# Two value blocks in one PSUM bank, and a norm's last square written to PSUM

## The chip, the cores and the metric

The kernel runs on one core of one Trainium2 chip. The metric is the device time of one execution in microseconds; lower is better. Several executions are timed and their median is given. Separately, one execution is taken with the hardware profiler, and the profile and the trace come from that one.

## The reference

Two layers of a bidirectional encoder over 512 tokens of width 1024, in float32. Each layer has three residual blocks, each behind an RMS norm:

```python
for l in range(DEPTH):
    x = x + hybrid_mixer(rms_norm(x, norm_mix[l]), w_in[l], ...)
    x = x + memory_cross_attention(rms_norm(x, norm_mem_q[l]), rms_norm(mem, norm_mem_kv[l]), ...)
    x = x + conv_ffn(rms_norm(x, norm_ffn[l]), w_up[l], conv_w[l], conv_b[l], w_down[l])
return rms_norm(x, norm_final)

def rms_norm(x, g):
    return x * lax.rsqrt(jnp.mean(x * x, axis=-1, keepdims=True) + EPS) * g
```

The mixer projects the normalised tokens once (`proj = h @ w_in`) into queries, keys and values. Eight heads of width 64 attend to a window of a 2-D grid of tokens (the neighbourhood heads), eight query heads on two key heads attend to all tokens (the grouped heads). One output product joins both. The memory block attends to 256 memory tokens with four heads, and the last block is a gated feed-forward layer with a convolution of width 3 over the positions.

## The kernel before

**Layout.** The tokens are kept transposed: `xT[c]` is a tile of 128 features by 512 tokens, and c runs over KC = 8 chunks. A product in float32 precision is made of three matmuls of a faster type: every operand is split into a hi part (a cast by ScalarE, ACT) and a lo part (the difference), and `mm3` adds hi x hi, hi x lo and lo x hi into one PSUM bank. So every weight that is loaded, and every result that is multiplied again, is split: ACT casts, and VectorE (DVE) or GpSimd (POOL) subtracts. Weights are split on line 742 (hi, ACT) and line 743 (lo, POOL, in a few cases DVE).

**PSUM.** There are eight banks of 128 x 512 values, given out in turn from three pools: four `mm` banks for products (`ps_mm`), two `sc` banks for scores (`ps_s`), two `tr` banks for transposes and small sums (`ps_t`). A tile of a pool takes the bank of the tile that came as many turns before, and has to wait until that one was used for the last time.

**A norm.** `Norm` does not wait for its statistic. Each closing product of the block before gives one chunk of the new x; `close` adds it into x (lines 978, 979), makes the split operands `xg` for the next product with the gain alone (lines 987, 989), and squares the chunk on ACT (line 995). POOL adds the squares up in SBUF, but the last chunk's (c = 7) is added by DVE (line 1006). `stat` then sums over the partitions with eight small matmuls (`tr<-ones,t`), and the rest of rsqrt follows on DVE (line 944) and POOL (line 946). `spread` brings rstd into a row form, and the results of the products are scaled with it when they are evicted (lines 1215, 1220 for q and k, lines 1037 and 1038 for the values). The very first norm, on the input, is built apart, with its squares added by DVE. The final norm has no gain column (`gcol is None`).

**The first products of a layer.** Their order is `NA_ORDER`: q and k of head pair 0, q and k of pair 1, then the value blocks of the first four heads (`project_v`), q and k of pairs 2 and 3, then one wide product for the other values and the keys of the grouped heads (`kv`), and one for their queries (`gq`). q and k of pair 0 use `sc` banks, all others `mm` banks. In layer 0 the three first products run interleaved while the input lands. `project_v` makes four blocks of 128 tokens by 256 columns; for each it takes one `mm` bank, of which it uses half, runs 24 matmuls and evicts the block with `split_v`. When all four are done, `straddle` copies halves of them by DMA into blocks that lie across the borders.

**The order of work.** The program is written as generators that a `Filler` interleaves, and PE's work is traced in that order. Then `Order` plans ACT, DVE, POOL and PE anew: it makes 30 rounds of a list schedule with estimated times, moves due times after each round by a seeded random draw, keeps the round that ended first, and pins the order of every engine to it. Transfers on SP's queue stay in the written order. In its estimates, DVE and POOL exclude each other where an operation "shares", and a DVE operation that reads a PSUM tile does not:

```python
if self.engine != "DVE" or what not in ("InstTensorTensor", "InstTensorScalarPtr") or self.banked(self.reads):
    return False
```

Two operations of different engines on one PSUM bank are kept one after the other, whichever columns they touch.

Of the kernel before, what the change touches and what calls it, by code (L numbers as in the profile page):

```python
# [19 lines left out]
P = 128  # L20
# [6 lines left out]
KC = D // P  # L27
# [628 lines left out]
def encoder_kernel(ctx: ExitStack, tc: tile.TileContext, t: dict, out: bass.AP):  # L656
# [17 lines left out]
    def nm(s):  # L674
        uid[0] += 1
        return f"{s}_{uid[0]}"
# [15 lines left out]
    def tmp(shape=(S,)):  # L692
        return tpool.tile([P, *shape], F32, tag="t", name=nm("t"))
# [4 lines left out]
    def ps(tag, bufs):  # L698
        return psum.tile([P, S], F32, tag=tag, name=nm(tag), bufs=bufs)

    ps_mm = lambda: ps("mm", 4)
    ps_s = lambda: ps("sc", 2)
    ps_t = lambda: ps("tr", 2)
# [91 lines left out]
    def get_w(key, ahead=AHEAD):  # L795
        n = done[0]
        assert plan[n][0] == key, (plan[n][0], key)
        prepare_w(1 + ahead)
        done[0] += 1
        w = ready[n]  # L800
        ready[n] = None
        return w
# [89 lines left out]
    def mm3(ps, ah, al, bh, bl, start, stop, **k):  # L892

        PE.matmul(ps, ah, bh, start=start, stop=False, **k)
        PE.matmul(ps, ah, bl, start=False, stop=False, **k)
        PE.matmul(ps, al, bh, start=False, stop=stop, **k)
# [66 lines left out]
    class Norm:  # L963
# [27 lines left out]

        def square(self, c, act=ACT, eng=None):

            sq = tmp((self.n,)) if self.gcol is not None or c == 0 or c >= KC - 2 else ps_s()[:, : self.n]
            e = act.activation(sq, xT[c][:, self.cols], AF.Square)
            eng = eng or (POOL if self.gcol is not None and c < KC - 1 else DVE)
            if self.acc is None:
                self.acc = sq
            elif c >= KC - 2 and self.gcol is None:
                self.last.append(sq)  # L1000
            elif c == 1:
                acc = tmp((self.n,))
                eng.tensor_add(acc, self.acc, sq)
                self.acc = acc
            else:
                eng.tensor_add(self.acc, self.acc, sq)  # L1006
            return e
# [24 lines left out]
    def split_psum(hi, lo, ps, scale=None):  # L1032
        if scale is None:
            ACT.copy(hi, ps)  # L1034
            DVE.tensor_sub(lo, ps, f(hi))  # L1035
        else:
            ACT.mul(hi, ps, scale)
            DVE.scalar_tensor_tensor(lo, ps, scale, f(hi), op0=ALU.mult, op1=ALU.subtract)
# [114 lines left out]
    for l in range(DEPTH):  # L1153
# [100 lines left out]
        vblk, straddled = [None, None], [False, False]  # L1254

        def v_blocks(g):
            vs = [rtile((2, 4, P)) for _ in range(4)]
            vblk[g] = {P * b: vs[b // 2][:, b % 2] for b in range(NB)}
            vblk[g].update({P * b + 64: vs[2 + b // 2][:, b % 2] for b in range(NB - 1)})
            return vs  # L1260
# [24 lines left out]
        def project_v(g):  # L1285

            w = [get_w(("v", g, kh)) for kh in range(2)]
            vs = v_blocks(g)
            for b in range(NB):
                pm = ps_mm()[:, :256]  # L1290
                bs = slice(b * P, b * P + P)
                for k in range(KC):
                    wh, wl = (v[:, k % 4, :] for v in w[k // 4])
                    mm3(pm, xg[k][0][:, bs], xg[k][1][:, bs], wh, wl, k == 0, k == KC - 1)
                    if k == 3:
                        yield
                split_v(vblk[g][P * b], pm, b)
                if b == NB - 1:
                    late(1, lambda: straddle(g, vs))
                yield  # L1300

        def split_v(v, pm, b):
            split_psum(v[:, :, 0:HD], v[:, :, HD:P], pm.rearrange("p (h d) -> p h d", d=HD), mix.rstd[:, b : b + 1])
# [17 lines left out]
        def straddle(g, vs):  # L1321
            straddled[g] = True
            for dst, src in (
                (vs[2][0:64, 0:2], vs[0][64:128, 0:2]),
                (vs[2][64:128, 0], vs[0][0:64, 1]),
                (vs[2][64:128, 1], vs[1][0:64, 0]),
                (vs[3][0:64, 0], vs[1][64:128, 0]),
                (vs[3][64:128, 0], vs[1][0:64, 1]),
            ):
                SP.dma_start(f(dst), f(src))  # L1330
# [311 lines left out]
        if l > 0:  # L1642
            load_bias(0)
        project = {"v": project_v, "kv": project_kv, "gq": lambda p: project_gq()}
        units = [project[n](p) if n in project else project_qk(n, p) for n, p in NA_ORDER]
        nns = []
# [444 lines left out]
```

## Time and profile before

| what | us |
|---|---|
| median of 3 runs | 1319.31 (1319.14 to 1320.14) |
| the profiled execution, its own time | 1318.48 |
| its span in the profile | 1316.7 |
| TensorE (PE) busy | 1303.8 |
| DVE busy | 1003.9 |
| ACT busy | 786.6 |
| POOL busy | 721.2 |

The granted TensorE clock is 0.999 of full speed. A row of the timeline has the start and the time in us, the engine, the line, the operation, the tiles (out<-in, without numbers), the shape and a count, and in brackets how long the engine was idle before it and what ended that. `tr<-ones,t` are the sums of a norm, `mm<-xg,hi` and `mm<-xg,lo` a projection, `mm<-hi,xg` and `mm<-lo,xg` a product in which the tokens are the stationary side, as in the value blocks. All matmuls stand under line 103, the helper that counts them.

### The profile page before, as it was taken

The page shows a single profiled execution, that of the slowest core. Times are in us where ns is not written, and L with a number is a line of the kernel's source. Part 1 is how long each engine was busy: PE and PEld are TensorE (multiplying, and loading weights), DVE is VectorE, ACT ScalarE, POOL GpSimd, SP SyncE. Part 2 cuts the span into 40 slices and gives each one's busy share as a digit, 9 for nine tenths or more (in the row PEclk, how much of TensorE's full clock was granted, in tenths as well). Part 3 has the DMA queues.
Part 4 walks back from the last instruction along what each step waited for, and adds up shares of the span by engine and source line. Part 5 has one row for each costly group of instructions (what it writes and reads, how often), then busy time and mean ns, then how long its engine had stood idle before and what let it go on. Part 6 is the DMA issues. An engine that isn't in the chain of part 4 may idle for free.

```text
span 1316.7 us, 21053 instructions
## 1 busy us (share of the span) xinstructions
PE 1303.8 (99%) x7632; PEld 1146.9 (87%) x7632; DVE 1003.9 (76%) x1858; ACT 786.6 (60%) x1458; POOL 721.2 (55%) x520
## 2 busy tenths in 40 slices
PE   9999999999999999999999999999999999999998
PEld 8888888888789999999888888888887999999987
DVE  6569877665999987788545688876759999877874
ACT  6768876555645555545536678765645555555544
POOL 3657966717464454445736569655454544444443
PEclk9999999999999999999999999999999999999999
DMA  7744322313223333333455523223222333333332
GB/s 239 199 118 134 97 80 65 96 48 112 75 70 105 109 108 101 97 95 102 138 147 166 146 78 100 62 78 95 64 84 85 88 90 105 105 98 90 110 104 76
DMA packets 205000, 136.98 MB, mean 104 GB/s; under 512 B 5600, under 2 KB 195040, under 8 KB 204896
## 3 DMA queue, kind: packets, MB, share of 16 engines
q1 hardware_dynamic: 204080, 134.98, 35.2%
q8 instruction: 60, 0.98, 0.3%
q10 hardware_dynamic: 816, 0.66, 0.2%
q14 instruction: 44, 0.36, 0.1%
HBM read 125.65 MB, written 2.10 MB: 97 GB/s over the span
## 4 chain that ended last, share of the span: by engine, by line
PE 89%; DVE 6%; ACT 2%; issue 1%; DMA 1%; POOL 0%; SPq 0%; POOLq 0%; DVEq 0%; ACTq 0%
PE mm L103 61%; PE sc L103 20%; PE tr L103 4%; PE tr L1537 2%; DVE t L1830 1%; DMA xT<-in_xT 1%; DVE t L1006 1%; PE tr L1382 1%; DVE r L1850 1%; PE tr L1724 1%; DVE r L1035 1%; DVE xg L1859 0%; DVE r L1252 0%; ACT t L1360 0%; ACT r L1034 0%
## 5 line engine op out<-in xcount | busy, mean ns | idle before, releaser
L743 POOL TENSOR_TENSOR lo<-raw,hi 128x512 fp32r<-128x512 f32 (+3 forms) x230 | 370.5, 1624 | 288.5 <-ACT hi L742 238.2
L103 PE MATMUL mm<-r,hi 128*128 128x512 f32 (+1 forms) x1392 | 396.5, 366 | 0.0
L103 PEld LDWEIGHTS mm<-r,hi 128*128 128x128 f32 x1392 | 245.3, 189 | 34.8
L103 PE MATMUL mm<-xg,hi 128*128 128x512 f32 (+1 forms) x960 | 267.3, 363 | 1.1 <-DVE xg L1859 0.3
L103 PE MATMUL mm<-r,lo 128*128 128x512 f32 (+1 forms) x728 | 257.5, 356 | 0.0
L742 ACT CAST hi<-raw 128x512 fp32r<-128x512 f32 (+3 forms) x234 | 167.8, 740 | 133.3 <-PE mm L103 45.3
L103 PEld LDWEIGHTS mm<-xg,hi 128*128 128x128 f32 x960 | 170.1, 189 | 30.2 <-DVE xg L1859 2.7
L103 PE MATMUL mm<-xg,lo 128*128 128x512 f32 (+1 forms) x480 | 173.5, 361 | 0.0
L103 PE MATMUL sc<-r,hi 128*128 128x256 f32 (+1 forms) x832 | 162.6, 291 | 0.0
L754 POOL TENSOR_TENSOR lo<-sf,hi 128x1024 fp32r<-128x1024 f32 x32 | 77.6, 2426 | 148.3 <-ACT hi L751 112.1
L103 PEld LDWEIGHTS mm<-r,lo 128*128 128x128 f32 x728 | 137.5, 189 | 19.8
L103 PEld LDWEIGHTS sc<-r,hi 128*128 128x128 f32 x832 | 133.8, 191 | 4.9
L103 PE MATMUL sc<-r,lo 128*128 128x256 f32 (+1 forms) x416 | 121.1, 291 | 0.0
L751 ACT CAST hi<-sf 128x1024 fp32r<-128x1024 f32 x64 | 67.2, 1049 | 86.7 <-DVE sf L766 47.2
L103 PE MATMUL mm<-hi,xg 128*128 128x512 f32 (+1 forms) x384 | 111.3, 360 | 1.3 <-DVE r L1252 1.3
L103 PEld LDWEIGHTS mm<-xg,lo 128*128 128x128 f32 x480 | 90.7, 189 | 13.8
L754 POOL TENSOR_TENSOR lo<-raw,hi 128x1024 fp32r<-128x1024 f32 x32 | 77.5, 2422 | 44.5 <-PE mm L103 25.0
L1041 POOL TENSOR_SCALAR t<-t,s 128x512 f32<-128x512 f32 (+1 forms) x112 | 66.5, 607 | 48.9 <-DVE s L1521 25.5
L103 PEld LDWEIGHTS sc<-r,lo 128*128 128x128 f32 x416 | 79.6, 191 | 1.2
L103 PEld LDWEIGHTS mm<-hi,xg 128*128 128x128 f32 x384 | 68.0, 190 | 10.5 <-DVE r L1252 1.5
L103 PE MATMUL sc<-r,r 128*128 128x256 f32 (+1 forms) x352 | 74.3, 330 | 0.0
L765 DVE TENSOR_TENSOR sf<-raw 128x512 f32<-128x512 f32 x32 | 62.7, 1960 | 8.2 <-DMA raw<-in_w_up 8.2
(200 smaller groups left out, 2629.6 us busy)
## 6 DMA issues: line engine op xcount, KB each, us to landing
raw<-in_w_up SPq DMA_DIRECT2D x88, 512.0 KB, 3.8
raw<-in_w_down SPq DMA_DIRECT2D x36, 384.0 KB, 3.5
raw<-in_w_in SPq DMA_DIRECT2D x25, 512.0 KB, 4.8
raw<-in_w_mem_kv SPq DMA_DIRECT2D x16, 512.0 KB, 4.3
raw<-in_w_down SPq DMA_DIRECT2D x24, 320.0 KB, 3.1
r<-in_bias SPq DMA_DIRECT2D x16, 384.0 KB, 5.3
r<-r SPq DMA_DIRECT2D x22, 256.0 KB, 3.4
raw<-in_w_in SPq DMA_DIRECT2D x18, 256.0 KB, 4.7
```

What stands on the lines that cost most here:

```text
L103: return self.engine.matmul(out, lhsT, rhs, **k)
L742: act.copy(hi[:, k], raw[:, k])
L743: (POOL if eng[0] == "P" else DVE).tensor_sub(lo[:, k], raw[:, k], f(hi)[:, k])
L751: act.copy(hi, src)
L754: eng.tensor_sub(lo[:, c], src[:, c], f(hi)[:, c])
L765: DVE.tensor_add(both[:, :4], raw[:, :4], raw[:, 4:])
L1006: eng.tensor_add(self.acc, self.acc, sq)
L1035: DVE.tensor_sub(lo, ps, f(hi))
L1041: eng.tensor_scalar(e, e, sums[:, col : col + 1], 1.0, op0=ALU.mult, op1=ALU.mult)
L1382: PE.transpose(tr[:, (2 * i + c) * P : (2 * i + c + 1) * P], es[j][:, i, c * P : (c + 1) * P], ident)
L1537: PE.transpose(tr[:, k * P : (k + 1) * P], es[j][:, k * P : (k + 1) * P], ident)
L1724: PE.transpose(tr[:, (2 * c + i) * P : (2 * c + i + 1) * P], e[:, i, c * P : (c + 1) * P], ident)
```

## The change

In `square`, the square of the last chunk is written to a `tr` bank in place of an SBUF tile, in every norm with a gain column but the very first. There are five of these: the memory norm and the feed-forward norm of both layers and the mixer norm of layer 1. In `project_v`, blocks 0 and 1 share one `mm` bank, and so do blocks 2 and 3; both blocks of a pair are evicted after the second is complete.

```diff
         def square(self, c, act=ACT, eng=None):
-            sq = tmp((self.n,)) if self.gcol is not None or c == 0 or c >= KC - 2 else ps_s()[:, : self.n]
+            if self.gcol is not None and eng is None and c == KC - 1:
+                sq = ps_t()
+            else:
+                sq = tmp((self.n,)) if self.gcol is not None or c == 0 or c >= KC - 2 else ps_s()[:, : self.n]
             e = act.activation(sq, xT[c][:, self.cols], AF.Square)
...
             for b in range(NB):
-                pm = ps_mm()[:, :256]
+                if b % 2 == 0:
+                    bank = ps_mm().rearrange("p (i c) -> p i c", i=2)
+                pm = bank[:, b % 2]
                 bs = slice(b * P, b * P + P)
                 for k in range(KC):
                     wh, wl = (v[:, k % 4, :] for v in w[k // 4])
                     mm3(pm, xg[k][0][:, bs], xg[k][1][:, bs], wh, wl, k == 0, k == KC - 1)
                     if k == 3:
                         yield
-                split_v(vblk[g][P * b], pm, b)
+                if b % 2:
+                    for i in range(2):
+                        split_v(vblk[g][P * (b - 1 + i)], bank[:, i], b - 1 + i)
                 if b == NB - 1:
                     late(1, lambda: straddle(g, vs))
                 yield
```

## The prediction

> **What bounds the kernel now.** I read the page first, then who waited for whom on PE, then busy time by stage, and last the timeline around the two longest waits. The page:
>
> ```profile
> span 1316.7 us, 21053 instructions
> ...
> PE 1303.8 (99%) x7632; PEld 1146.9 (87%) x7632; DVE 1003.9 (76%) x1858; ACT 786.6 (60%) x1458; POOL 721.2 (55%) x520
> ```
>
> TensorE is busy for all but 12.9 us, and the change takes no matmul away. So it can only win idle time of PE, or lose some. Where that idle time lies, by stage (the columns: stretch, its length, busy time of PE, PEld, DVE, ACT and POOL):
>
> ```profile
> 33.00:38.00 5.00, 3.73 (x31) 3.53 (x30) 3.09 (x6) 4.86 (x9) 0.00 (x0) 1.00 0.33 93
> 38.00:320.00 282.00, 281.26 (x1485) 238.03 (x1484) 200.39 (x453) 190.91 (x422) 185.05 (x169) 1.00 0.36 103
> 320.00:660.00 340.00, 339.59 (x2129) 307.07 (x2128) 284.86 (x443) 186.09 (x276) 173.52 (x89) 1.00 0.35 102
> 660.00:663.00 3.00, 1.71 (x10) 1.17 (x9) 3.00 (x2) 1.14 (x2) 1.94 (x2) 1.00 0.66 175
> 663.00:965.00 302.00, 301.11 (x1600) 255.65 (x1600) 205.87 (x464) 196.46 (x429) 181.34 (x165) 1.00 0.35 102
> 965.00:1284.00 319.00, 318.33 (x2034) 289.40 (x2033) 268.65 (x423) 171.74 (x251) 156.13 (x75) 1.00 0.33 97
> 1284.00:1316.70 32.70, 26.52 (x204) 25.32 (x203) 15.42 (x37) 15.43 (x36) 12.64 (x10) 0.97 0.22 76
> ```
>
> Two short stretches, 33 to 38 us and 660 to 663 us, lose 1.27 and 1.29 us. The four long ones lose 0.74, 0.41, 0.89 and 0.67 us, together 2.71 us in 1243 us. The rest is the tail (6.2 us) and the start, and neither edit works there. PE's own waits name the two short stretches (in total, times, longest):
>
> ```profile
> PE tr L103 <- DVE t L1006: 1.3, 1, 1.3
> PE mm L103 <- DVE r L1252: 1.3, 1, 1.3
> PE tr L1382 <- DVE r L1252: 0.8, 2, 0.6
> ```
>
> The first is a norm's column sums (`tr<-ones,t`) waiting for the last addition of squares, line 1006. The second is a product into an `mm` bank waiting for the lo part of a q tile, line 1252. Each of the two edits touches one of them.
>
> **The norm's last square.** This is layer 1's first norm, on the timeline:
>
> ```profile
> 656.88 5.05 POOL L743 TENSOR_TENSOR lo<-raw,hi 128x512 fp32r<-128x512 f32 x4
> ...
> 658.10 0.75 DVE L989 SCALAR_TENSOR_TENSOR xg<-mm,par,xg 128x512 fp32r<-128x512 f32 x1 [0.76 <-ACT xg L987]
> ...
> 658.76 3.72 DVE L1006 TENSOR_TENSOR t<-t,t 128x512 f32<-128x512 f32 x1
> ...
> 660.40 0.62 PE L103 MATMUL sc<-xg,hi 128*128 128x512 f32 x2
> 660.86 0.39 PE L103 MATMUL sc<-xg,lo 128*128 128x512 f32 x1
> ...
> 662.54 1.05 PE L103 MATMUL tr<-ones,t 128*128 128x1 f32 x8 [1.29 <-DVE t L1006]
> ```
>
> POOL runs four weight splits back to back, 1.26 us each, from 656.88 to 661.93. DVE's addition of two SBUF tiles starts inside that run, takes 3.72 us and ends 0.55 us after the run, at 662.48. The DVE operation just before it, 0.75 us at 658.10, lies inside the same run and is not stretched; it has one large SBUF input, its other comes from PSUM. The other additions of this line and of its likes:
>
> ```profile
> L1006 DVE TENSOR_TENSOR t<-t,t 128x512 f32<-128x512 f32 x11 | 13.1, 1193 | 11.3 <-POOL t L1006 10.3 <-ACT t L80 0.5
> L978 DVE TENSOR_TENSOR mm<-mm,xT 128x512 f32<-128x512 f32 x32 | 21.7, 693 | 12.4 <-PE mm L103 12.4
> L995 ACT ACTIVATE sc<-xT 128x256 f32<-128x256 f32 x10 | 3.9, 388 | 4.2 <-DVE xT L1974 4.0
> L995 ACT ACTIVATE t<-xT 128x256 f32<-128x256 f32 x6 | 2.5, 418 | 2.0 <-DVE xT L1974 1.8
> ```
>
> With the square in PSUM the addition has the form of line 978, PSUM with SBUF: mean 693 ns over 32, so none is stretched much. It would end at 658.76 + 0.69 = 659.45. PE's matmuls before the sums start every 0.23 us (660.40, two of them, then 660.86), so the sums could start at 660.86 + 0.23 = 661.09 instead of 662.54: 1.45 us less. (The profile shows 1.29, because it models the end of a matmul later than the next one can start.) What would be late next is PE's own order, with 1.6 us of slack.
>
> Here a rule is weighed against the row. The row: the addition came when the second of the four splits was running, and was held to the end of the fourth. The Trainium skill, page SBUF — State Buffer, section "Who interferes with whom", says that a VectorE operation with two SBUF inputs and a GpSimd operation that reads SBUF exclude each other, and that the first to issue holds the ports for one instruction. By that the addition would have gone after the second split, at 656.88 + 2 x 1.26 = 659.40, ended near 660.1, and PE would have lost nothing; the edit would be worth 0. The row decides: three splits were waited for.
>
> The edit is in four more norms. There the addition isn't stretched:
>
> ```profile
> 252.23 0.69 DVE L1006 TENSOR_TENSOR t<-t,t 128x512 f32<-128x512 f32 x1 [2.22 <-POOL t L1006]
> ...
> 254.11 0.95 PE L103 MATMUL tr<-ones,t 128*128 128x1 f32 x8
> ```
>
> It ends at 252.92 and PE comes 1.2 us later without a wait; the other three have no row among PE's waits either. Worth 0, and if that cover of 1.2 us were gone, 0.03 us of ScalarE time each (418 against 388 ns at half width). The square takes one turn more in the two `tr` banks. The bank it gets was last used by work that its own input depends on (transposes or the up product before the closing products), and the third tile in turn, the spread of rstd, comes after the addition. So no wait is added: 0.
>
> **The two value blocks.** Layer 0, where the second wait lies:
>
> ```profile
> 34.55 1.17 ACT L1250 CAST r<-mm 64x512 fp32r<-64x512 f32 x2
> 35.54 0.28 PE L103 MATMUL mm<-lo,xg 128*128 128x256 f32 x1
> 35.66 0.28 PE L103 MATMUL mm<-hi,xg 128*128 128x256 f32 x1
> 35.76 1.39 DVE L1252 TENSOR_TENSOR r<-mm,r 64x512 fp32r<-64x512 f32 x2 [1.83 <-ACT r L1250]
> 36.95 0.47 ACT L1037 ACTIVATE r<-mm,s 128x256 fp32r<-128x256 f32 x1
> 37.20 0.39 PE L103 MATMUL mm<-hi,xg 128*128 128x256 f32 x1 [1.27 <-DVE r L1252]
> 38.62 0.48 DVE L1038 SCALAR_TENSOR_TENSOR r<-mm,s,r 128x256 fp32r<-128x256 f32 x1
> ```
>
> The four `mm` banks hold q1, k1, value block 0 and value block 1; block 2 needs q1's bank, which DVE empties at 37.15. From 35.66 to 37.20 is 1.54 us, where these matmuls start every 0.12 us: 1.42 us lost. After the change blocks 0 and 1 take the third bank, 2 and 3 the fourth, and block 2 starts at 35.78. The next to need q1's bank is q2, after two whole blocks (43.06 - 37.20 = 5.86 us by the rows here and below), at 41.64, 4.5 us after it is empty. What is late next, then:
>
> ```profile
> 41.47 1.30 POOL L743 TENSOR_TENSOR lo<-raw,hi 128x512 fp32r<-128x512 f32 x1
> 43.06 0.63 PE L103 MATMUL mm<-xg,hi 128*128 128x512 f32 x2
> 44.34 0.48 DVE L1038 SCALAR_TENSOR_TENSOR r<-mm,s,r 128x256 fp32r<-128x256 f32 x1 [1.58 <-ACT r L1037]
> 45.09 3.44 SPq L80 DMA_DIRECT2D r<-r  x5
> 68.69 1.12 PE L103 MATMUL mm<-r,r 128*128 128x256 f32 x8
> ```
>
> The second half of q2's lo is there at 42.77 and wanted 12 matmuls of 0.23 us after 41.64, at 44.4: 1.6 us to spare. Blocks 0 and 1 are now evicted only after block 1. Before, block 0 was already waiting for ACT until 36.95, so this delays little; the four steps of a pair in a row are 2 x (0.47 + 0.48) = 1.9 us. Behind them stand the five copies that make the straddling blocks, in SP's queue with weight loads after them. The last pair ends near 41.6 + 1.9 = 43.5, plus hand-overs, where the copies start at 45.09 now; the first values product is at 68.69. The cover is over 20 us: 0. In layer 1 PE has no wait of this kind: 0.
>
> **The sum.** Against the profiled execution (1318.48 us, span 1316.7): 1318.48 - 1.45 - 1.42 = 1315.61. It ran 0.83 us below the median of the runs, 1319.31, so on the median 1316.4, -0.22%. Everything else is planned anew, since the planner orders each engine by a search that the first difference sends another way. The bound for that from the rows: the idle 2.71 us of the long stretches could go to nothing or double. I take 0 for it and keep both ends.
>
> **The rivals.** *One gain is absorbed (1317.9).* In the chain of waits of layer 0, in order of time, the stretch between these two pieces is nearly all DVE's:
>
> ```profile
> 117.53 1.29 DVE r L1035 x2
> ...
> 135.91 0.43 DVE t L1408
> ```
>
> DVE is nearly gapless there. Had it a beat of its own, 1.42 us earlier at PE would be given back: 1319.31 - 1.45 = 1317.9. Against it, that run of DVE was itself started by PE:
>
> ```profile
> 110.54 1.29 DVE L1440 TENSOR_TENSOR t<-mm,r 128x512 f32<-128x512 f32 x2 [0.84 <-PE mm L103]
> ...
> 136.52 1.59 DVE L1084 SCALAR_TENSOR_TENSOR r<-r,par,r 128x256 fp32r<-128x256 f32 x1
> ```
>
> so it should move with PE. Chance 0.13.
>
> *The addition stays blocked (1317.9).* It still reads and writes an SBUF tile; if that is enough to be held, only 1.42 us is won: 1319.31 - 1.42. Against it the unstretched 0.75 us at 658.10, which reads and writes SBUF too. By the rule of the Trainium skill above, under which POOL's run did not make PE wait, the edit would bring nothing, and the result would be this one as well. Chance 0.12.
>
> *The new order puts other additions behind runs of POOL (slower, 1322.5).* The block of 658.76 cost DVE 3.72 - 0.69 = 3.03 us; line 1084 at 136.52 (1.59 us) shows that an SBUF-only operation is also held in the stretch that DVE bounds, where PE follows it one for one. One block of 3.03 us there cancels the gain (1319.31 - 2.87 + 3.03 = 1319.5, no change), chance 0.08; from the second on it is slower, 1322.5, chance 0.10. For it: the planner knows nothing of the old block either, or it would not have made it. Against it: one such wait reached PE in the whole program.
>
> **How the numbers follow.** A measurement of this kernel can tell about 0.2%, 2.64 us, from no change: the lines are 1316.67 and 1321.95. The forecast, 1316.4 with 0.57, lies next to the first of them; re-planning moves it either way, and I give a little over two thirds of it to the faster side (0.40), the rest to no change (0.17). Of the two absorbed cases, one in five comes below the line by the same lottery (0.05, leaving 0.20). One block adds 0.08 to no change. Faster 0.45, same 0.45, slower 0.10. For the range, the lower end is the forecast less two thirds of the 2.71 us, 1314.6; the upper end takes in the absorbed cases and the single block, 1320.0, and leaves out the slower rival and some of the luck below.
>
> **What would show it.** Right: no wait of PE for line 1006 near 660 us and none for line 1252 near 36 us; line 1006 with a PSUM input at about 0.69 us in all five norms; value blocks 2 and 3 following 0 and 1 without a gap; PE's idle time down from 12.9 to near 10 us. Wrong: line 1006 again over 1 us while POOL runs; a PE wait for line 1037 or 1038 (a shared bank held too long); SP's copies later than 45 us; or the idle time of the four long stretches grown by more than 2.7 us, over DVE operations with two SBUF inputs.

## The result, and the profile after

| | median, us | runs | ratio to before | 95% interval |
|---|---|---|---|---|
| before, on the same chip | 1318.91 (1316.18 to 1321.05) | 22 | | |
| after | 1315.84 (1314.52 to 1318.82) | 22 | 0.998 | 0.9973 to 0.9986 |

The change wins 3.07 us, 0.23%; the whole interval lies below 1. The first profiled execution of the changed kernel ran 1318.82 us, 3 us above its median. A second profile of the same kernel (it is called *both, again* below) ran 1315.81. By the starts of the same PE instructions the first lost 2.3 us against the second between 20 and 30 us, 0.7 of them in a longer wait in the first norm and the rest right behind it, where TensorE's clock dropped, and 1.2 us more near 75 us. Rows of both are shown, and which is which is said each time.

The page of the first profile:

```profile
span 1317.0 us, 21049 instructions
...
PE 1304.5 (99%) x7632; PEld 1148.2 (87%) x7632; DVE 998.9 (76%) x1858; ACT 786.8 (60%) x1458; POOL 722.1 (55%) x520
```

DVE has lost 5 us of busy time (1003.9 before), 3.03 of them the one stretched addition. PE's own work is the same. Its busy time by stage, first profile (after the stretch and its length: PE, PEld, DVE, ACT, POOL; then the granted clock):

```profile
0.00:33.00 33.00, 30.74 (x135) 25.52 (x136) 20.68 (x32) 19.15 (x33) 10.59 (x13) 0.95 0.79 237
33.00:38.00 5.00, 5.00 (x44) 5.00 (x44) 4.23 (x7) 3.78 (x7) 0.00 (x0) 1.00 0.40 108
38.00:320.00 282.00, 279.89 (x1483) 237.11 (x1482) 200.69 (x454) 192.84 (x425) 183.34 (x168) 1.00 0.37 103
320.00:660.00 340.00, 338.55 (x2123) 306.08 (x2122) 281.53 (x441) 183.88 (x272) 173.57 (x88) 1.00 0.34 101
660.00:663.00 3.00, 3.00 (x15) 2.49 (x14) 2.04 (x4) 2.24 (x4) 3.00 (x3) 1.00 0.51 170
663.00:965.00 302.00, 301.73 (x1607) 256.60 (x1605) 206.56 (x463) 197.26 (x431) 183.20 (x167) 1.00 0.36 104
```

Both short stretches are full now: 5.00 of 5.00 where it was 3.73, and 3.00 of 3.00 where it was 1.71. But two long stretches have more idle time than before: 2.11 us in 38 to 320 (0.74 before), 1.45 in 320 to 660 (0.41 before); 663 to 965 has less (0.27, before 0.89). PE's longest waits behind the start, first profile:

```profile
PE mm L103 <- DVE r L1238: 1.6, 1, 1.6
PE tr L103 <- DVE t L1009: 0.9, 1, 0.9
PE mm L103 <- ACT r L1037: 0.9, 1, 0.9
```

The two waits named in the prediction are gone, and three others stand there. (In this kernel line 1009 is the line 1006 of before, and 1238 the line 1235 of `split_k`, which writes the lo part of a k tile.) The second is in the very first norm, at 25.5 us, which the change does not touch. The first one matters: it is at 75.49 us, in layer 0, right behind the value blocks. In the second profile it is 0.4 us, and the wait in the first norm 0.2. The third, at 381.66, is most of what the stretch from 320 to 660 us has lost.

The norm itself on the timeline of the first profile, and the group of line 1009 (count, then busy us and mean ns):

```profile
659.63 3.81 POOL L743 TENSOR_TENSOR lo<-raw,hi 128x512 fp32r<-128x512 f32 x3
...
660.65 0.59 ACT L998 ACTIVATE tr<-xT 128x512 f32<-128x512 f32 x1
...
661.46 0.68 DVE L1009 TENSOR_TENSOR t<-t,tr 128x512 f32<-128x512 f32 x1
```

```profile
L1009 DVE TENSOR_TENSOR t<-t,tr 128x512 f32<-128x512 f32 x5 | 3.4, 687 | 5.7 <-POOL t L1009 5.7
```

POOL's run lies beside the addition as before, and the addition takes 0.68 us. All five have the mean of 687 ns.

### The profile page after: what moved, and what is told of

It reads as the page before. It is cut to its first block, busy times and chain, and to the rows that moved or that the text cites. A ratio compares the mean times of both kernels' runs of the same rounds, so it can differ in the third digit from the quotient of the medians.

```text
span 1317.0 us, 21049 instructions
## 1 busy us (share of the span) xinstructions
PE 1304.5 (99%) x7632; PEld 1148.2 (87%) x7632; DVE 998.9 (76%) x1858; ACT 786.8 (60%) x1458; POOL 722.1 (55%) x520
## 4 chain that ended last, share of the span: by engine, by line
PE 90%; DVE 5%; ACT 2%; issue 1%; POOL 1%; DMA 1%; SPq 0%; POOLq 0%; DVEq 0%; ACTq 0%
PE mm L103 61%; PE sc L103 21%; PE tr L103 4%; PE tr L1544 2%; DVE t L1837 1%; DMA xT<-in_xT 1%; PE tr L1389 1%; DVE r L1857 1%; PE tr L1731 1%; DVE t L1009 1%; DVE xg L1866 0%; POOL lo L743 0%; DVE r L1879 0%; DVE r L1038 0%; PE tr L1459 0%
## 5 line engine op out<-in xcount | busy, mean ns | idle before, releaser
L103 PEld LDWEIGHTS mm<-hi,xg 128*128 128x128 f32 x384 | 68.2, 190 | 10.7 <-DVE r L1238 1.9
L103 PE MATMUL mm<-lo,xg 128*128 128x512 f32 (+1 forms) x192 | 68.7, 358 | 0.0
```

The lines of the kernel that those rows point to most:

```text
L103: return self.engine.matmul(out, lhsT, rhs, **k)
```

## Where the time goes: one table over all traces

To compare traces I took the start of the same PE instruction in each, and how its distance to another such instruction differs from the profile of before. Three stretches hold the story. "Pairs" runs from the first matmul of the value blocks to the first scores (29.14 to 45.81 us in the profile of before), "load" from there to the first `mm<-ones,t` (94.74), "square" from the first `tr<-xg,hi` (383.66) to the sums of layer 1's first norm (662.54). "Old order" is a kernel in which ACT, DVE, POOL and PE are pinned to the order that was planned for the kernel before, "new order" to the one planned for the changed kernel. So edits and order could be put together freely. "Light" kernels come further below. The first four columns are one profiled execution of each kernel, the median and the ratio are of its runs.

| kernel (us against before) | pairs | load | square | end of span | median | ratio to before, interval |
|---|---|---|---|---|---|---|
| after | -1.53 | +1.61 | -1.45 | +0.31 | 1315.84 | 0.998 (0.9973 to 0.9986) |
| both, again | -1.53 | +0.37 | -1.45 | -2.68 | 1315.82 | 0.9968 (0.9954 to 0.9982) |
| square, old order | -0.01 | +0.87 | -1.45 | -1.00 | 1317.14 | 0.9985 (0.9964 to 1.0006) |
| pairs, old order | -1.53 | +3.31 | 0.00 | +1.06 | 1318.87 | 1.0003 (0.9985 to 1.002) |
| both, old order | -1.52 | +2.92 | -1.45 | -0.67 | 1318.89 | 0.9993 (0.9978 to 1.0008) |
| neither, new order | +0.59 | -0.33 | -0.04 | +0.83 | 1320.00 | 1.0005 (0.999 to 1.0019) |
| square, new order | +2.08 | -0.32 | -1.45 | -0.43 | 1317.29 | 0.9974 (0.9957 to 0.999) |
| pairs, new order | -1.53 | +1.66 | 0.00 | -0.71 | 1318.22 | 0.9981 (0.9964 to 0.9998) |
| light, neither edit | -0.02 | -0.32 | 0.00 | -0.57 | 1317.74 | 0.9991 (0.9976 to 1.0006) |
| light, pairs | -1.52 | -0.33 | 0.00 | -0.48 | 1317.64 | 0.999 (0.9978 to 1.0003) |
| light, both | -1.52 | -0.33 | -1.45 | -3.88 | 1314.46 | 0.9958 (0.9944 to 0.9971) |

The kernel before ran at 1318.87 beside the three old-order kernels and the one with neither edit, at 1320.12 beside the other three of the new order, at 1319.62 beside the first two light ones and at 1319.85 beside the last. These four groups ran on four chips, so a kernel is best compared within its group or by its ratio.

## The experiments

### Each edit in the old order, and both

```diff
 # Order.data, pinned kernels
-        best, kept_credit, self.credit, draw = None, {}, {}, random.Random(SEED)
-        for n in range(ROUNDS):
...
+        can, best = self.canonical(), [0.0, {}]
+        for e, v in json.loads(zlib.decompress(base64.b85decode(GIVEN))).items():
+            at, mine = 0, []
+            for d in v:
+                at += d
+                mine.append(self.steps[can[e][at]])
+            best[1][e] = mine
```

`GIVEN` holds the order of every engine as it was planned for the other kernel. With the change of `square` alone, of `project_v` alone, and with both. The square alone:

> Only the norm's last square goes to PSUM; every engine keeps the order that was planned for the kernel before. Theory (each edit takes away its own wait of PE, and the time passes through): the addition near 659 us takes 0.69 us instead of 3.72, PE's wait before the column sums goes, 1.45 us faster than before, near 0.9989 of it; the wait near 37 us stays. Rival (the gain comes from the newly planned order, the edits themselves do little): no change, 1.000. Rival (an addition that writes SBUF is still held): 3.7 us again near 659 us, 1.000.

The value blocks alone:

> Only the value blocks share banks in pairs; every engine keeps the order that was planned for the kernel before. Theory (each edit takes away its own wait): the third value block follows the second without a gap near 36 us, 1.42 us faster, near 0.9989 of before, and the scores that follow start 1.4 us earlier. Rival (absorbed where DVE is gapless, 110 to 136 us): the gain is there at 70 us and gone at 140 us, 1.000 in all. Rival (the gain comes from the new order): 1.000.

Both:

> Both edits, with every engine in the order that was planned for the kernel before. Theory (each edit takes away its own wait, nothing else matters): 1.45 + 1.42 = 2.87 us faster, 0.9978 of before, as the changed kernel itself; the idle time of PE in the other stretches as in the kernel before, without the new waits near 75 and 382 us. Rival (the new order brings the gain): 1.000.

In the trace the square does exactly its 1.45 us, in this order and in every other. The pairs also do what was worked out, 1.53 us, and then lose it twice over by 95 us, so that in the old order they are worth nothing (1318.87, and 1318.89 with both). Of the theories, the square's fits (1.73 us by the medians, though the interval still takes in 1), and those of the pairs and of both fell. The pairs' rival had looked for the loss between 110 and 136 us; it lies before 95. The chain of waits of the pairs alone shows what takes it, in order of time (start, us, what):

```profile
43.09 7.60 DMA r<-in_bias
50.69 0.02 issue
50.71 6.55 DMA raw<-in_w_in
...
57.36 1.14 ACT hi L747 x2
...
73.85 0.70 DVE r L1240
74.56 0.04 issue
74.60 1.43 PE mm L103 x5
```

and PE's row there:

```profile
74.60 0.50 PE L103 MATMUL mm<-hi,xg 128*128 128x512 f32 x1 [2.44 <-DVE r L1240]
```

The bias loads land late, SP issues the next weight load only then, ACT's cast of that weight waits 7.1 us for it, and everything behind the cast in ACT's and DVE's queues (exponentials, the casts and differences of q and k) comes out at the eviction of k3, whose `mm` bank PE wants at 74.60. From the cast to that product it is a fixed distance. In the kernel before:

```profile
56.23 1.15 ACT L742 CAST hi<-raw 128x512 fp32r<-128x512 f32 x2 [3.78 <-DMA raw<-in_w_in]
...
73.47 0.19 PEld L103 LDWEIGHTS mm<-hi,xg 128*128 128x128 f32 x1 [0.29 <-DVE r L1235]
```

73.47 - 56.23 = 17.24, and 74.60 - 57.36 = 17.24. The square alone and both edits in this order have the same distance (73.95 - 56.71 and 74.33 - 57.10). So before the change PE arrived at this point just as the eviction was done. Whatever is won ahead of it is lost there, unless the load comes earlier too. (The 3.31 us of the pairs hold 0.65 by which that execution had started earlier, lost at the same place.) The load came 1.1 us later instead. The transfers were slower (the busy share of the 16 DMA engines and GB/s are the last two columns), in the kernel before and in the pairs alone; why they were slower is not shown:

```profile
48.00:52.00 4.00, 4.00 (x19) 3.31 (x18) 1.14 (x4) 3.97 (x13) 2.04 (x3) 1.00 1.04 276
52.00:56.00 4.00, 4.00 (x23) 3.48 (x22) 2.21 (x4) 0.45 (x1) 2.45 (x4) 1.00 1.09 272
```

```profile
48.00:52.00 4.00, 4.00 (x19) 3.32 (x18) 1.69 (x4) 2.26 (x5) 3.64 (x5) 1.00 1.04 234
52.00:56.00 4.00, 4.00 (x23) 3.45 (x22) 2.33 (x9) 0.00 (x0) 0.28 (x1) 1.00 0.99 226
```

### The new order without edits, with each, and with both again

> Neither edit, but every engine in the order that was planned for the changed kernel. Theory (the edits bring the gain, the new order costs what the changed kernel's trace shows: 1.8 us more idle time of PE in the long stretches): both waits of PE are there again, near 37 us about 1.4 us, and the addition of squares near 660 us is held wherever POOL's splits stand beside it; 1.0 to 2.0 us slower than before, 1.001. Rival (the new order brings the gain): about 3 us faster, 0.998, as the changed kernel.

> The changed kernel once more, for a second profile. In its first profile PE's wait near 36 us was gone, but 1.6 us was lost again near 75 us, behind a weight load that ScalarE waited for until 59 us. Theory (layer 0 up to 75 us runs at the pace of the loads on SP's queue, so the block edit brings nothing there): ScalarE again waits over 4 us for a load near 56 to 59 us, and the product into an mm bank near 75 us waits over 1 us. Rival (that was chance of one execution): no wait over 0.5 us near 75 us. Both: 0.998 of before.

> Only the norm's last square goes to PSUM, every engine in the order planned for the changed kernel; against the changed kernel it lacks the shared banks alone. Theory (the loads set the pace of layer 0): as fast as the changed kernel, 0.998 of before, though PE waits 1.4 to 1.9 us near 37 us, because the wait near 75 us is shorter by that. Rival (each edit passes its gain through): 1.4 us slower than the changed kernel, 0.999 of before.

> Only the value blocks share banks, every engine in the order planned for the changed kernel; against the changed kernel it lacks the PSUM square alone. Theory and rival alike: the addition near 660 us is held by POOL's splits, 1.3 to 1.9 us slower than the changed kernel, 0.999 to 1.000 of before. If it is not held in this order, as fast as the changed kernel.

The new order by itself brings nothing (1320.00 beside 1318.87; ratio 1.0005, 0.999 to 1.0019). With it the square alone is 2.8 us faster, the pairs alone 1.9 and both 4.3, each against the 1320.12 of the kernel before in its company. Two theories fell. The square alone was not as fast as the changed kernel but 1.5 us slower, and the second profile has no wait of over 1 us near 75 us, though ACT again waits 4.79 us for a load. The pairs alone were 2.4 us slower than the changed kernel, where 1.3 to 1.9 had been expected. What the new order does for the pairs is seen at the same point. Second profile of the changed kernel, then the first:

```profile
56.09 0.63 ACT L742 CAST hi<-raw 128x512 fp32r<-128x512 f32 x1 [4.79 <-DMA raw<-in_w_in]
...
72.19 0.50 PE L103 MATMUL mm<-hi,xg 128*128 128x512 f32 x1 [0.41 <-DVE r L1238]
```

```profile
59.41 0.62 ACT L742 CAST hi<-raw 128x512 fp32r<-128x512 f32 x1 [6.06 <-DMA raw<-in_w_in]
...
75.49 0.50 PE L103 MATMUL mm<-hi,xg 128*128 128x512 f32 x1 [1.63 <-DVE r L1238]
```

72.19 - 56.09 = 16.10 us, and 75.49 - 59.41 = 16.08; the pairs alone have 73.05 - 56.96 = 16.09. The planner's new order has 1.15 us less work between the load and this product. How much of the pairs' gain gets through still hangs on when the load lands: 0.37 us is lost in one of these three profiles, 1.61 and 1.66 in the other two. By the medians 1.5 us gets through on top of the square (1317.29 to 1315.82). The rest of the new order is give and take in the second profile: 0.59 won by 254 us, 1.32 lost by 384 and 1.07 won between 669 and 902.

With the pairs alone in the new order, DVE's additions of squares on the timeline:

```profile
659.00 3.79 DVE L1011 TENSOR_TENSOR t<-t,t 128x512 f32<-128x512 f32 x1
...
897.63 2.87 DVE L1011 TENSOR_TENSOR t<-t,t 128x512 f32<-128x512 f32 x1
...
958.60 2.88 DVE L1011 TENSOR_TENSOR t<-t,t 128x512 f32<-128x512 f32 x1 [0.60 <-POOL t L1011]
```

So in that order all three norms of layer 1 have a held addition, where the old order has one. The two later ones stand beside one split of 128x1024 each, which takes 2.4 us, and cost PE nothing. With the square in PSUM all are at 0.69.

### Lighter transfers

```diff
-                SP.dma_start(bias[p][j][:, 0:3, :], t["bias"][l, 2 * p + j])
+                SP.dma_start(bias[p][j][:, 0:1, :], t["bias"][l, 2 * p + j][:, 0:1])
...
-                        out=sc[j][:, i, :], in0=sc[j][:, i, :], in1=bias[p][j][:, WTYPE[b], :],
+                        out=sc[j][:, i, :], in0=sc[j][:, i, :], in1=bias[p][j][:, 0, :],
```

In the old order, without an edit, with the pairs, and with both. These kernels leave out two of the three bias slabs, so only their times are of use.

> The kernel before, in its own order on every engine, but each bias load brings one of its three slabs (128 KB instead of 384 KB) and every block uses that one, so the first layer's first 60 us carry about 1 MB less. Theory (the weight load for which ACT waits until 56 us is late because of the bytes ahead of it on the same queue): ACT's wait for it, 3.8 us in the kernel before, shrinks to under 2 us; PE has few other waits there, so the time itself falls by no more than 1.5 us (1317.5 to 1319). Rival (the load is late because its buffer or the issuing engine is late, not because of bytes): ACT's wait stays within 0.7 us of 3.8 and the time is the kernel's before.

> The same light bias loads and the same old order, with the value blocks in pairs. Theory (the 1.5 us won at 36 us are lost again near 75 us because the weights and the k3 eviction behind them keep the pace of the loads): with light loads there is no PE wait near 75 us above 0.5 us, the 1.5 us are still there at 95 us, and the time is 1.2 to 1.8 us under that of the same kernel without pairs. Rival (the loss comes from the pair itself: ACT and DVE get the second block later and everything queued behind it moves): PE waits 1.5 us or more for the k3 eviction near 75 us here as well, and the two light kernels are within 0.5 us of one another.

> Both edits in the old order of every engine, with the same light bias loads (one slab of three, used for every block). With the full loads these two edits in this order gave 1318.9 us, no less than the kernel before; the light loads alone gave 1317.74, with pairs 1317.64. Theory (the pairs' 1.5 us are given back near 75 us only because the transfer stream paces the weights there, and the square's 1.46 us stand by themselves): PE has no wait over 0.5 us near 75 us, and the time is 1314.4 to 1315.2 us. Rival (light loads do not protect the pairs, as the medians of the two light kernels, 0.1 us apart, suggest): a wait near 75 us or another of its size by 95 us, and 1316.0 to 1316.6 us, the square's share alone.

In the trace the theory holds in all three. The bias loads land in 3.9 to 4.5 us (medians) in place of 6.2 before and 8.2 with the pairs, and ACT's cast no longer waits for the weight but for PE, in the kernel without edits too. With both edits:

```profile
53.03 1.14 ACT L747 CAST hi<-raw 128x512 fp32r<-128x512 f32 x2 [2.52 <-PE mm L103]
...
69.50 1.41 DVE L1243 TENSOR_TENSOR r<-mm,r 64x512 fp32r<-64x512 f32 x2 [1.46 <-ACT r L1239]
...
71.25 0.48 PE L103 MATMUL mm<-hi,xg 128*128 128x512 f32 x1
```

The product that waited at 74.60 starts at 71.25 without a wait, the pairs' 1.52 us stay won, and the time is 1314.46 us, 3.28 below the light kernel without edits (3.5 if each is taken against the kernel before beside it): in the same old order in which the same two edits with full loads brought nothing. Its five runs lie within 0.33 us (1314.35 to 1314.68), where those of before spread over 3.

One number does not fit: the medians of the first two light kernels are only 0.1 us apart, where the trace says that 1.5 us are kept. The profiled execution of the pairs lost 1.8 us before 12 us, where its first projection began 0.75 us later (5.15 for 4.40) and ran at half rate for longer: the full clock came at 10.3 us, in the light kernel without edits at 6.6. First the light kernel without edits, then with pairs:

```profile
6.76 1.31 PE L103 MATMUL sc<-xg,hi 128*128 128x512 f32 x5
```

```profile
7.58 2.33 PE L103 MATMUL sc<-xg,hi 128*128 128x512 f32 x5
```

The pairs do not touch that place. Whether the other runs lost there too isn't known, and why this median is not lower stays open. The third light kernel speaks for the trace, since its 3.28 us are more than the square's 1.45; but a light kernel with the square alone was not run, so the pairs' share of them was not measured by itself.

### A stretched addition by itself

> Leaves out the whole computation. It measures by itself how a VectorE addition of 128x512 fares when GpSimd runs 1, 2, 4 or 6 subtractions of SBUF tiles back to back, about 1.27 us each. One ScalarE copy releases both engines; VectorE first adds into PSUM (0.69 us), then adds either two SBUF tiles or an SBUF and a PSUM tile. Theory (held to the end of the run): the addition of two SBUF tiles ends about 0.55 us after the last subtraction, whatever their number, so it takes about 1.1, 2.4, 5.0 and 7.5 us; with a PSUM input 0.69 us in all. Rival (held for one instruction, then it takes its turn): about 1.1 to 1.3 us for every number.

> Leaves the whole computation out. One addition on VectorE of two SBUF tiles (128x512) behind 2, 3, 4 or 6 VectorE instructions that read PSUM, beside six GpSimd subtractions back to back; in every second trial the instruction just ahead of the addition is a scalar_tensor_tensor with one PSUM and one SBUF operand, as in the kernel. So the addition becomes ready in the first to fourth subtraction of the run. Theory (it waits for at most one GpSimd instruction, whenever it comes): 0.7 to 1.9 us in all eight. Rival (a run that is already under way is not broken into: the addition waits for its end, which the first probe missed because it came during the run's first instruction): 1.25 us where it comes in the first subtraction, and the rest of the run, 3.5 to 6 us, where it comes in the second or later, as the 3.7 us of the kernel's norm. Third: only behind the scalar_tensor_tensor is it held.

First probe, four GpSimd operations, then the worst row of the second, six of them:

```profile
18.01 1.25 DVE L23 TENSOR_TENSOR acc<-acc,y 128x512 f32<-128x512 f32 x1
...
24.63 0.68 DVE L23 TENSOR_TENSOR acc<-acc,pv 128x512 f32<-128x512 f32 x1
```

```profile
5.20 7.81 POOL L25 TENSOR_TENSOR lo<-x,y 128x512 fp32r<-128x512 f32 x6 [4.76 <-ACT y L25]
6.50 1.74 DVE L25 TENSOR_TENSOR acc<-acc,y 128x512 f32<-128x512 f32 x1
```

With a PSUM operand the addition takes 0.68 us beside any run of POOL. With two SBUF operands it took 1.25 us beside two, four or six operations, and between 0.68 and 1.74 us in the eight arrangements of the second probe. So it waits for one GpSimd operation at most, wherever it comes in the run and whatever stood ahead of it: that a run is held to its end fell, as the theory of the first probe and as a rival in the second. The Trainium skill states that the shared ports are held for the whole of one instruction (SBUF — State Buffer, "Who interferes with whom"), and both probes agree with it. In the kernel the addition was nevertheless held for 3.72 to 3.79 us in all six profiles that have it there with SBUF operands.

It is not that a full kernel as such holds it. In the very first norm of the kernel before, additions of the same line run beside splits of the same line:

```profile
17.95 7.15 DVE L1006 TENSOR_TENSOR t<-t,t 128x512 f32<-128x512 f32 x6 [0.47 <-ACT t L80]
...
21.12 5.11 POOL L743 TENSOR_TENSOR lo<-raw,hi 128x512 fp32r<-128x512 f32 x3 [2.35 <-ACT hi L742]
```

The additions at 21.81 and 23.51 take 1.60 us each and the splits 1.7 us in place of 1.26: there the two engines take turns, as in the probes. Casts on ACT run beside the first of these two additions as they do near 659 us, but no transfers (0 GB/s from 21.1 to 22.9 us; 152 from 658.7 to 662.5). What makes the difference near 659 us stays open.

## Why the prediction was right, and where it was lucky

**The bound: right.** PE's work did not change, and all that was won or lost is idle time of PE.

**The norm's last square, -1.45: right to the hundredth.** The square stretch is 1.45 us shorter in all six profiles with the edit, within 0.04 of unchanged in the five without, and the addition takes 0.68 us. That the old addition is held through three splits was read off one row. The row was right for this place in all six profiles; the rule is right in the probes and in the first norm of the same trace, whose rows the prediction did not weigh. So the price was right and the mechanism behind it was not known. The 0 for the other four norms holds for PE, but only in the old order was there nothing to hide.

**The value blocks, -1.42: the wait right, the cover wrong.** The pairs win 1.53 us wherever they are. The step that failed is the statement of what is late next. I followed the `mm` bank to q2 and the copies to the first values product, and found 20 us of cover. The copies do go out at 44.6 us in the second profile (47.2 in the first, which ran late), and no wait of PE names them. But I did not ask whom PE meets next if it comes 1.4 us earlier: at 73.47 it met an eviction that had just been done, on a chain that begins at a weight load and moves with the transfers, not with PE. Two rows of the trace said so, ACT's 3.78 us of waiting at 56.23 and PEld's 0.29 at 73.47, and the prediction used neither.

**Re-planning, 0: wrong in kind, right in sum.** It was costed as a lottery beside the edits. It is nothing by itself (ratio 1.0005), but by the medians it is what lets the pairs through. In the old order the change would have been no change at all: 1318.89. So that 1316.4 was near 1315.84 is in part luck: two zeros were wrong in opposite directions. Of the 0.56 us between the two, 0.40 lie in the kernel before, whose median was 1319.31 in the first three runs and 1318.91 in all 22.

**The rivals.** "One gain is absorbed" named the right thing at the wrong place: not DVE's stretch from 117 to 136 us but the loads behind 43 us, and in the changed kernel it takes 0.4 to 1.6 of the 1.5 us. "The addition stays blocked" fell with the 0.68 us. "Other additions behind POOL" did not show: five additions at a mean of 687 ns.

**Medians beyond the trace.** 3.07 us of median is about the sum of the two terms, 2.87, although 0.4 to 1.6 of it is given back; the next section has what may stand against that. PE's idle time, 12.9 us before, is 12.5 in the first profile and 10.7 in the second, where "near 10" was forecast.

## What the runs showed of the hardware

A short wait of PE can cost more than itself. In three of the twelve profiles of the table and of before, the granted clock dropped to half for 3.41 us right after such a wait; between 11 and 1284 us it did so nowhere else. In the square-only kernel in the new order PE waits 1.87 us at 37.28; stage by stage:

```profile
38.00:42.00 4.00, 4.00 (x24) 4.00 (x23) 2.92 (x5) 1.62 (x4) 3.69 (x4) 0.57 0.35 70
42.00:46.00 4.00, 4.00 (x30) 3.76 (x29) 0.10 (x1) 2.27 (x5) 1.96 (x3) 1.00 0.97 279
```

24 matmuls in a stretch where the kernel before has 36: 1.49 us more than the wait cost the same order without edits (2.08 against 0.59). That kernel's twelve runs fall into two groups, six at 1316.3 to 1316.8 with a mean clock of 0.999 and six at 1317.7 to 1318.5 with 0.997 or 0.998, about 1.5 us apart. Beside its faster half the pairs are worth only 0.6 us in this order (1316.4 to 1315.82), beside its slower half 2.2. The other two drops: the neither kernel in the new order, after a 1.25 us wait for the held addition, lost 1.6 us between 663 and 669 (clock 0.63 in 664 to 668); and the first profile of the changed kernel, after 0.92 us in the first norm:

```profile
26.76 0.97 PE L103 MATMUL mm<-xg,hi 128*128 128x512 f32 x2
27.52 0.63 PE L103 MATMUL mm<-xg,lo 128*128 128x512 f32 x1
27.95 1.06 PE L103 MATMUL mm<-xg,hi 128*128 128x512 f32 x2
```

27.52 to 27.95 is 0.43 us for one matmul, where the kernel before starts one every 0.23. Other profiles have waits of the same length and no drop. What else differs can be counted. In all twelve traces the changes of the clock lie whole multiples of 3.41 us apart. In the windows of this grid matmuls worth 14.5 of 512 columns start (median); in the three windows ahead of the drops it was about 5, 5 and 6. Three more windows with 5 or 6 were followed by no drop (near 70 us in the old order with pairs and with both, and near 661 us with pairs), and no fuller window was followed by one. So what counts seems to be how little work one window holds, rather than how long the wait is, and even then it struck in three of six. The Trainium skill (TensorE: Matmul & The Clock Gate, "What's actually happening") tells of a free-running activity window of about 3.4 us that halves the clock after an idle window; length and halving agree with these rows, but here a partly idle window was enough. So a wait that is taken away also takes away a chance to lose 1.5 us more. That fits the narrow spread of the light kernel with both edits, whose PE waits 0.5 us at the longest in layer 0 behind the start, and the medians that gain more than the traces; how often it strikes was not measured.

## What to carry to other kernels

Where a wait of the bounding engine is removed, ask next whom that engine meets with its new lead: look for the first row behind it where it waits a little or arrives just in time, and follow that chain back. If it begins at a transfer that the chain waits for, the lead is lost there unless the transfer moves as well. And give a re-planned order its own column: with one pinned order for all variants, an edit's gain and what the order does to it can be told apart.
